# Issuing five of six first loads behind the frame's barriers, and waiting for the last stores on SyncE

## The chip, the core and the metric

The kernel runs on one core of a Trainium2 chip. The metric is the device time of one execution in microseconds; lower is better. Times "before" are from four executions. A profile is one of them, recorded by the hardware profiler; its instants are counted from the first instruction of the program.

## The reference

Attention scores without the softmax: for each of 8 batches and 8 heads, the 512 x 512 products of the rows of q and k (64 long), times 1/8.

```
batch, heads, seq, dim = 8, 8, 512, 64          # float32
scale = 1.0 / np.sqrt(q.shape[-1])
out = np.einsum('bhqd,bhkd->bhqk', q, k) * scale
```

q and k are 8.4 MB each, the output is 67.1 MB.

## The kernel before, in words

The batch is cut into four units of two batches (`UNITS = 4`). For each unit, k and q are loaded whole, 2 MB each, by `load(v, x)` (L77, x = 0 for k, 1 for q), into one of three large buffers `bigs`. GpSimd casts each load to bf16 in two instructions (L119), in the order of the loads, and counts `ready` up once per load. TensorE transposes the cast data in groups of eight tiles (`turn`, L127), VectorE and ScalarE each move half of every group into `kT` and `qz` (`move`, L185). `qz` was filled with zeros by VectorE at the start (L190).

The output is made in 16 pieces of 4 MB (`ALL = 16`, index g). For each, TensorE does eight pairs of matmuls into three PSUM buffers (`scores`, L142), ScalarE (L210) and VectorE (L213) take turns scaling them into one of the three `bigs`, and SyncE issues one store of the whole piece (L96). From the fourth piece on, TensorE waits for the store that used the same buffer three pieces before.

All DMAs are issued by SyncE on one queue, in this order: the six loads of units 0 to 2, the two loads of unit 3 (each after a count of `ready`, L91), and the 16 stores (each after counts of `act` and `dve`, L94 and L95). Each load has its own semaphore; the stores share three.

The instructions are put out by hand, engine by engine. A frame of the scheduler, `tile_critical` (L82), encloses what is issued first. `tc.close()` and `tc.compile()` (L86, L87) end the frame: there all engines meet at barriers. What is written after L87 starts on each engine behind them: GpSimd's identity and casts, VectorE's fills, ScalarE's table load, and SyncE's list from L90 on. At the end of the program one engine waits on the three store semaphores, so that the program does not end before its output has landed.

Of the kernel before, what the change touches and what calls it, by code (L numbers as in the profile page):

```python
# [5 lines left out]
def kernel(  # L6
# [5 lines left out]
    nc = tc.nc  # L12
# [3 lines left out]
    UNITS = B // 2  # L16
# [23 lines left out]
    store_sems = [nc.alloc_semaphore(f"store{n}") for n in range(3)]  # L40
    ALL = CHUNKS * UNITS
# [24 lines left out]
    pe = nc.tensor  # L66
# [3 lines left out]
    def xf(v):  # L70
        return bigs[(0, 1, 2, 1)[v]].rearrange("p x i k -> p (x i k)").rearrange(
            "p (x s c) -> p x s c", x=2, s=2)

    def store_buffer(g):
        return bigs[(0, 2, 1)[g % 3]]

    def load(v, x):  # L77
        nc.sync.dma_start(out=xf(v)[:, x],
                          in_=(k_r, q_r)[x][v].rearrange("p (s c) -> p s c", s=2)
                          ).then_inc(load_sems[2 * v + x], 16)  # L80

    with tc.tile_critical(no_gpsimd_drain=True):  # L82
        for v in range(UNITS - 1):
            for x in range(2):
                load(v, x)
    tc.close()  # L86
    tc.compile()  # L87


    for x in range(2):  # L90
        nc.sync.wait_ge(sem["ready"], 3 + x)  # L91
        load(UNITS - 1, x)
    for g in range(ALL):
        nc.sync.wait_ge(sem["act"], 4 * g + 4)  # L94
        nc.sync.wait_ge(sem["dve"], 4 * g + 4)  # L95
        nc.sync.dma_start(out=out_r[g], in_=store_buffer(g).rearrange("p x i k -> p x (i k)")  # L96
                          ).then_inc(store_sems[g % 3], 16)

    nc.gpsimd.memset(identity, 0.0).then_inc(sem["ident"], 1)  # L99
    nc.gpsimd.wait_ge(sem["ident"], 1)  # L100
# [51 lines left out]
    for g in range(ALL):  # L152
# [7 lines left out]
            scores(g, p)  # L160
        if c < ALL:
            pe.wait_ge(sem["moved"], 4 * c + 4)


    for n in range(3):
        pe.wait_ge(store_sems[n], 16 * len(range(n, ALL, 3)))

# [76 lines left out]
```

## Time and profile before

| what | value |
|---|---|
| median of 4 executions | 201.72 us (201.6 to 201.94) |
| the profiled execution | 201.94 us, span 200.4 us |
| busy share of the span | PE 50%, VectorE 53%, ScalarE 42%, GpSimd 20% |
| moved by DMA | 83.95 MB, mean 419 GB/s |
| six loads of the frame | issued from 0.95 to 3.47 us |
| the last store | issued at 178.05 us, landing in about 22 us |

The span runs from the first to the last instruction of the program; the execution's time has 1.57 us more around it (201.94 less 200.37). In the chain, each row is a piece of work that the next one waited for. A DMA row starts at its issue and ends at its landing, and so includes the time that the transfer stood in the queue behind others. "SPq" and "PEldq" are the sequencers of SyncE and TensorE: their issues, waits and drains.

### The profile page before, as it was taken

To read this page: it belongs to the slowest core of one execution; us is meant where nothing else is said; L and a number is where in the kernel's file an instruction comes from. 1 tells how busy PE (TensorE), PEld (TensorE's weight loads), DVE (VectorE), ACT (ScalarE), POOL (GpSimd) and SP (SyncE) were. 2 spreads that over 40 slices of the span, in tenths; PEclk is the share of its full clock that TensorE was granted. 3 is DMA by queue.
4 is the path that set the end of the run, shared out by engine and by line. 5 is a ranking of instruction groups with operands and counts; after the bars stand their busy time and mean duration, and the time that the engine had idled before them with its cause. 6 is when DMAs were issued, how large, how long until landed. Compare 5 with 4: busy or idle time off the path is not lost.

```text
span 200.4 us, 1081 instructions
## 1 busy us (share of the span) xinstructions
PE 99.4 (50%) x377; PEld 46.7 (23%) x384; DVE 106.2 (53%) x98; ACT 84.9 (42%) x97; POOL 39.5 (20%) x22
## 2 busy tenths in 40 slices
PE   0027550376686638745666666662757573820000
PEld 0026310142433215312333414130212120200000
DVE  0666790075798927692747493947363645450000
ACT  0205760264695726562646464554444443430000
POOL 0399999995000000000000000000000000000000
PEclk9999996588899966997978788899585769695555
DMA  5999999999999999999999999999999999999995
GB/s 186 428 438 425 435 425 438 428 406 435 432 428 425 428 443 430 425 425 442 428 425 425 435 442 425 425 435 435 425 428 428 438 425 422 435 432 428 425 428 242
DMA packets 5509, 83.95 MB, mean 419 GB/s; under 512 B 384, under 2 KB 384, under 8 KB 384
## 3 DMA queue, kind: packets, MB, share of 16 engines
q1 hardware_dynamic: 5504, 83.89, 98.4%
q8 instruction: 3, 0.05, 0.1%
q14 instruction: 2, 0.02, 0.0%
HBM read 16.78 MB, written 67.11 MB: 419 GB/s over the span
## 4 chain that ended last, share of the span: by engine, by line
DMA 53%; DVE 12%; POOL 12%; PE 10%; issue 1%; SPq 0%
DMA out_dram<-big 42%; POOL xb L119 12%; DVE big L213 10%; DMA big<-in_q_dram 7%; PE ps L142 7%; DMA big<-in_k_dram 4%; PE tp L127 3%; DVE qz L185 2%; DVE kT L185 1%; SPq L95 0%; SPq L87 0%; SPq L82 0%
## 5 line engine op out<-in xcount | busy, mean ns | idle before, releaser
L142 PE MATMUL ps<-kT,qz 128*128 128x512 bf16 x249 | 80.3, 457 | 62.4 <-DMA out_dram<-big 30.8
L213 DVE TENSOR_SCALAR big<-ps 128x1024 f32<-128x1024 f32 x64 | 77.1, 1223 | 52.7 <-PE ps L142 49.4
L210 ACT ACTIVATE big<-ps 128x1024 f32<-128x1024 f32 x64 | 65.1, 1025 | 71.9 <-PE ps L142 67.8
L142 PEld LDWEIGHTS ps<-kT,qz 128*128 128x128 bf16 x256 | 25.7, 111 | 110.4 <-DMA out_dram<-big 34.3
L119 POOL CAST xb<-big 128x2048 bf16<-128x2048 f32 x16 | 38.8, 2467 | 3.4 <-DMA big<-in_k_dram 3.1
L127 PE MATMUL tp<-identity,xb 128*128 128x128 f32 x104 | 19.8, 355 | 13.7 <-POOL xb L119 13.7
L127 PEld LDWEIGHTS tp<-identity,xb 128*128 128x128 f32 x104 | 17.9, 190 | 17.6 <-issue 16.3
L185 DVE COPY kT<-tp 64x512 f32<-64x512 f32 x14 | 9.7, 694 | 7.3 <-PE tp L127 6.9
L185 ACT COPY kT<-tp 64x512 f32<-64x512 f32 x14 | 8.1, 579 | 12.1 <-PE tp L127 11.9
L190 DVE MEMSET qz<- 128x4096 uint32 x2 | 6.9, 3472 | 6.7 <-PEq L87 5.9
L185 DVE COPY qz<-tp 64x512 f32<-64x512 f32 x12 | 8.3, 695 | 3.8 <-PE tp L127 3.5
L185 ACT COPY qz<-tp 64x512 f32<-64x512 f32 x12 | 7.4, 615 | 1.8 <-PE tp L127 1.6
L127 PE MATMUL ps<-identity,xb 128*128 128x128 f32 x24 | 3.9, 323 | 1.2 <-POOL xb L119 1.2
L127 PEld LDWEIGHTS ps<-identity,xb 128*128 128x128 f32 x24 | 3.5, 169 | 1.6 <-POOL xb L119 1.6
L185 ACT ACT_TABLE_LOAD x1 | 1.3, 1283 | 4.9 <-PEq L87 4.9
L185 DVE COPY qz<-ps 64x512 f32<-64x512 f32 x4 | 2.8, 695 | 0.9 <-PE ps L127 0.8
L185 ACT COPY qz<-ps 64x512 f32<-64x512 f32 x4 | 2.5, 624 | 1.1 <-PE ps L127 1.1
L185 DVE COPY kT<-ps 64x512 f32<-64x512 f32 x2 | 1.4, 693 | 0.3 <-PE ps L127 0.3
L185 ACT COPY kT<-ps 64x512 f32<-64x512 f32 x2 | 1.2, 579 | 0.5 <-PE ps L127 0.5
L99 POOL MEMSET identity<- 128x128 f32 x1 | 0.2, 205 | 4.5 <-POOLq L87 4.5
L101 POOL TENSOR_SCALAR_AFFINE_SELECT identity<-identity 128x128 f32<-128x128 f32 x1 | 0.3, 294 | 0.2 <-POOL identity L99 0.2
L230 POOL MEMSET const-float32-0.0<- 128x1 f32 x1 | 0.1, 99 | 0.2 <-issue 0.2
(3 smaller groups left out, 0.3 us busy)
## 6 DMA issues: line engine op xcount, KB each, us to landing
out_dram<-big SPq DMA_DIRECT2D x16, 4096.0 KB, 21.6
big<-in_k_dram SPq DMA_DIRECT2D x4, 2048.0 KB, 15.6
big<-in_q_dram SPq DMA_DIRECT2D x4, 2048.0 KB, 17.8
```

The source lines that it names most:

```text
L99: nc.gpsimd.memset(identity, 0.0).then_inc(sem["ident"], 1)
L101: nc.gpsimd.affine_select(out=identity, in_=identity, compare_op=mybir.AluOpType.not_equal, fill=1.0, base=0, pattern=[[-1, P]], channel_m ...
L119: cast = nc.gpsimd.tensor_copy(out=dst, in_=src)
L127: ins = pe.transpose(out=dst[:, w], identity=identity, in_=xw[:, c % SLOTS * W + w])
L142: ins = pe.matmul(out=pss[pair % 3][:, w, :], lhsT=qz[:, n, i + w], rhs=keys[:, n], start=True, stop=True)
L185: copy(out=dst, in_=src[:, h]).then_inc(sem["moved"], 1)
L190: engine.memset(qz[:, v * N:(v + 1) * N], 0.0).then_inc(sem["zeroed"], 1)
L210: lambda o, ps: nc.scalar.mul(out=o, in_=ps, mul=scale),
L213: lambda o, ps: nc.vector.tensor_scalar(out=o, in0=ps, scalar1=scale, scalar2=None, op0=mult),
L230: nc = _bacc.Bacc("TRN2", target_bir_lowering=False, num_devices=1)
```

## The change

Only `load(0, 0)` stays in the frame. The five other early loads are issued by SyncE after L87, in the same order, ahead of the loads of unit 3. The three waits for the last stores are taken from the end of TensorE's list and put at the end of SyncE's, after its last store.

```
     with tc.tile_critical(no_gpsimd_drain=True):
-        for v in range(UNITS - 1):
-            for x in range(2):
-                load(v, x)
+        load(0, 0)
     tc.close()
     tc.compile()
 
 
+    for n in range(1, 2 * (UNITS - 1)):
+        load(n // 2, n % 2)
     for x in range(2):
         nc.sync.wait_ge(sem["ready"], 3 + x)
         load(UNITS - 1, x)
@@ the stores
+    for n in range(3):
+        nc.sync.wait_ge(store_sems[n], 16 * len(range(n, ALL, 3)))
@@ the end of TensorE's list
-    for n in range(3):
-        pe.wait_ge(store_sems[n], 16 * len(range(n, ALL, 3)))
```

## The prediction

> **What bounds the kernel now.** I read the page first, then the chain of waits in order of time, then windows over the first microseconds, then SyncE's issues in order of time, and last the two source lines that the change touches, the end of the scheduler's frame (L87) and the closing waits (L166).
>
> From the page: the span, the DMA share in forty slices of 5.01 us, and the one queue that carries all loads and stores.
>
> ```profile
> span 200.4 us, 1081 instructions
> ...
> DMA  5999999999999999999999999999999999999995
> ...
> q1 hardware_dynamic: 5504, 83.89, 98.4%
> ```
>
> Every slice but the first and the last is full, and no compute engine is over 53% busy. So the kernel is one stream of 83.89 MB, and its time is a start-up, the stream, and an end. The chain (start us, duration us, what) says where both ends are.
>
> ```profile
> 0.95 7.78 DMA big<-in_k_dram
> 8.72 0.05 issue
> 8.78 4.82 POOL xb L119 x2
> ...
> 63.48 19.30 DMA out_dram<-big
> ...
> 90.11 21.96 DMA out_dram<-big
> ...
> 149.15 21.99 DMA out_dram<-big
> ```
>
> The stores that land at 63.48+19.30 = 82.78 and at 90.11+21.96 = 112.07 are three stores of 4.194 MB apart: 12.58 MB in 29.29 us, 430 GB/s. At that rate the stream alone is 83.89/0.430 = 195.1 us of the 200.4. What is left over is 5.3 us, so only the start-up and the end can give anything, unless the stream is broken.
>
> SyncE's issues (start us, duration us, line, transfer) and windows of the start-up (length, then busy us and count of PE, PEld, DVE, ACT, POOL, then clock, DMA share, GB/s):
>
> ```profile
> 0.95 0.38 SPq L78 DMA_DIRECT2D big<-in_k_dram  x1
> 1.38 0.42 SPq L78 DMA_DIRECT2D big<-in_q_dram  x1
> ...
> 3.47 0.47 SPq L78 DMA_DIRECT2D big<-in_q_dram  x1
> 23.44 0.33 SPq L78 DMA_DIRECT2D big<-in_k_dram  x1
> ```
>
> ```profile
> 0.00:2.00 2.00, 0.00 (x0) 0.00 (x0) 0.00 (x0) 0.00 (x0) 0.20 (x4) 1.00 0.09 33
> 2.00:4.00 2.00, 0.00 (x0) 0.00 (x0) 0.00 (x0) 0.00 (x0) 0.00 (x0) 1.00 0.94 238
> 4.00:6.00 2.00, 0.00 (x0) 0.00 (x0) 0.13 (x1) 1.05 (x1) 0.50 (x2) 1.00 0.98 418
> 6.00:8.00 2.00, 0.00 (x0) 0.00 (x0) 2.00 (x1) 0.23 (x1) 0.00 (x0) 1.00 1.01 434
> ```
>
> Data moves from about 1.9 us on (0.09 of 2 us is 0.18 us). From 2 to 4 us the DMA engines are 94% busy but pass 238 GB/s, against 434 later: (430-238) x 2 us = 0.38 MB, or 0.9 us of stream lost. That is also the stretch in which SyncE issues loads 2 to 5.
>
> Frame and end (count, durations in ns min/median/max, first and last start us):
>
> ```profile
> L87 SPq EVENT_SEMAPHORE  x2: 17/17/17, 4.5 to 4.9; - x2
> ...
> L166 PEldq EVENT_SEMAPHORE  x2: 51/4873/9695, 181.0 to 190.7; - x2
> ```
>
> SyncE leaves the barriers at 4.9 us; TensorE's last wait runs from 190.68 for 9.695 us, to 200.37, and it is the last instruction of the program. The landing record of the last store says 200.34: TensorE follows it by 0.03 us. This execution took 201.94 us, so 1.57 us lie outside its span. It is the highest of the four, whose median is 201.72; I sum differences and put them on the median. A difference under 0.2% (0.4 us) is about what a measurement of this kernel cannot tell from none.
>
> **The change part by part.** *Five loads move behind the barriers.* SyncE's last issue in the frame ends at 3.47+0.47 = 3.94 and the barriers at 4.9+0.02, so frame exit and barriers cost SyncE 0.98 us. In the changed kernel load 0 is still issued at 0.95 (nothing ahead of it changes) and ends at 1.33; the other engines wait at the barrier from 0.8 us on, so the barriers end at about 2.3. Loads 1 to 5 follow at the old pitch, (3.47-1.38)/4 = 0.52 us: 2.4, 2.9, 3.4, 4.0, 4.5, done at 4.9. Each comes 1.0 us later than now. Behind them on SyncE stand only the wait for `ready` 3 and the last two loads, at 23.44 and 28.32, so nothing queues up.
>
> Is the stream broken? Load 0 is 2.097 MB, 4.88 us at 430 GB/s; it starts at about 1.9, so it cannot be through before 6.8, and it lands at 0.95+7.78 = 8.73. Load 1 must have data ready by 6.8 at the earliest; from issue to first data load 0 takes 0.95 to 1.9, 1.0 us, so load 1 is ready at 3.4. The cover is 3.4 us, and load 5, needed at 8.73+4x4.88 = 28.2, has over 20. Cost: nothing. If the cover were gone, each microsecond missing would be a microsecond of time.
>
> *Does the 0.9 us lost from 2 to 4 us change?* This the trace of before cannot show, since the first data and the burst of issues come together. Bounds: nothing changes if the loss belongs to the first packets themselves, or if it only moves with the burst to 2.4 to 4.9; -0.9 us if the burst causes it and the later burst finds a stream that is running. An upper end: the window in which load 3,0 is issued (23.44, in a running stream, a single one) keeps 431 GB/s from 20 to 30 us, so an issue costs under 0.1 us there; five of them at most +0.3. I take 0, because the nearest row, that issue in a running stream, shows no price on data and so speaks against the burst as the cause.
>
> *Other engines start 2.6 us earlier.* GpSimd's identity (4.94), ScalarE's table load (4.95) and VectorE's two memsets (5.87 and 10.14, 3.47 each) move to about 2.3, 2.3 and 3.3. None gains: GpSimd's first cast waits for load 0 at 8.73, TensorE's first transposes at 13.7 for that cast pair, and the first evacuation at 15.72 for them. What the casts release, loads 6 and 7 at 23.44 and 28.32, is wanted only when load 5 lands, at about 33.2: 5 us of lead at the least. Store buffers come free by landings, which do not move. Cost 0.
>
> *The closing waits move from TensorE to SyncE.* Instructions: three waits, merged to two in the trace. On TensorE nothing stood behind them. On SyncE they stand behind the last store's issue (178.05, 0.37 us), with nothing behind them either. The last landing stays at 200.34, SyncE's semaphore instructions take 17 ns against 51, so the span ends within 0.05 us of now. What follows the last instruction, inside those 1.57 us, no row shows by engine. Today SyncE's share of it is run from 178.4 on, under 22 us of store, and TensorE's is exposed; afterwards the other way round. Bounds: -0.3 us if TensorE's is the longer by some ten semaphore steps of 34 ns; +0.6 us if SyncE has one more round of the kind that L87 shows (from its drain at 4.31 to 4.92). I take 0, since the rows nearest to it, single semaphore and drain instructions of 7 to 55 ns, are far under the resolution.
>
> [...]
>
> "DMA: Bandwidth & Descriptors", section "Rules for kernel authors", says to issue a DMA early and wait for it late, which speaks against delaying five loads; by that rule alone the change would cost up to 1.0 us, 202.7. The row of load 0 (landing 8.73, with load 1 issued at 2.4) decides against it here.
>
> Sum: 0 + 0 + 0 + 0 on 201.72: **201.7 us**.
>
> **The rivals.** *SyncE's end is longer (slower).* One mechanism: work behind the last instruction on SyncE that now hides under the last store is exposed. It decides from 0.4 us on; by the barrier row it is +0.4 to +0.7: 202.1 to 202.4. For it: 1.57 us lie outside the span, and SyncE is the engine with the queue. Against: single instructions there take tens of ns.
>
> *The start-up loss goes (faster).* The five issues caused the 0.9 us between 2 and 4 us, and with load 0 alone in the queue until 2.4 a good half is saved: -0.4 to -0.9, 200.8 to 201.3. For it: 94% busy at 238 GB/s, just while SyncE issues, and full rate from when it stops at 3.94. Against: the single issue at 23.44, without a dent, and the first packets would be slow in any case.
>
> *The change does not do what it says:* if SyncE were held in the frame until load 0 lands, load 1 would come at 9.5 and the stream would stop for over 1.5 us: above 203.2. Against: in the trace its drains there take 7 to 55 ns with six loads in flight.
>
> **How the numbers follow.** No change that can be told: 0.46. SyncE's longer end: 0.27. Start-up loss gone: 0.19. A held SyncE: 0.02. The rest, 0.06, is drift of the slowest DMA engine (the 16 parts of the last store land from 198.3 to 200.34, and the last one sets the time), split 0.04 faster and 0.02 slower. So faster 0.23, same 0.46, slower 0.31. The middle case alone is 201.3 to 202.1. The range takes in most of both rivals, 201.0 to 202.4, leaving out about 1 in 10 on each side.
>
> **What would show it right or wrong.** Right: load 0 at 0.95, loads 1 to 5 from about 2.4 to 4.9, casts still from 8.7 on, the last store's issue within 0.5 us of 178, a span of 200.2 to 200.6 ended by SyncE's wait. Wrong by the start: the window from 2 to 4 us well above 300 GB/s and the first cast before 8.3. Wrong by the end: the same span but more than 1.57+0.4 us outside it. A gap in the DMA share in the first two slices would mean that the cover of 3.4 us was miscounted.

## The result and the profile after

The changed kernel takes 201.45 us (median of 41 runs, 201.27 to 201.79), the kernel before 201.68 us (61 runs, 201.56 to 202.01). The ratio is 0.9987, 95% interval 0.9983 to 0.9992: faster by 0.13%, clear of noise over so many runs and inside the 0.2% that the prediction called no change. What is to be explained is 0.23 us.

The profiled execution took 201.78 us. Its page, lines that answer to those of before:

```profile
span 200.5 us, 1081 instructions
...
DMA  5999999999999999999999999999999999999995
...
q1 hardware_dynamic: 5504, 83.89, 98.4%
```

The span is not shorter (200.47 us against 200.37). The stream is as full as before. The chain of waits of the changed kernel (start us, duration us, what):

```profile
0.95 7.82 DMA big<-in_k_dram
8.76 0.05 issue
8.82 4.81 POOL xb L122 x2
...
148.52 22.71 DMA out_dram<-big
```

Load 0 is issued at the same instant, and the first cast starts 0.04 us later than before. SyncE's issues, and the window from 2 to 4 us:

```profile
0.95 0.39 SPq L78 DMA_DIRECT2D big<-in_k_dram  x1
2.34 0.34 SPq L78 DMA_DIRECT2D big<-in_q_dram  x1
...
4.29 0.46 SPq L78 DMA_DIRECT2D big<-in_q_dram  x1
23.46 0.33 SPq L78 DMA_DIRECT2D big<-in_k_dram  x1
```

```profile
2.00:4.00 2.00, 0.00 (x0) 0.00 (x0) 0.74 (x1) 1.28 (x1) 0.50 (x2) 1.00 0.96 254
```

Loads 1 to 5 come from 2.34 to 4.75, and the DMA engines still pass only 254 GB/s at 96% busy. Last, the closing waits, now on SyncE (count, ns min/median/max, first and last start in us):

```profile
L99 SPq EVENT_SEMAPHORE  x2: 17/4852/9686, 181.1 to 190.8; - x2
```

The second wait runs from 190.781 for 9.686 us, to 200.467, 0.02 us after the last landing at 200.444. What has changed is the time outside the span: 201.78 less 200.467 is 1.31 us, against 1.57 before. That is no accident of one run: over 42 runs of the changed kernel, the profiled one included, the time less the span is 1.305 us in the mean (1.26 to 1.38, with spans given to 0.1 us), and the mean span is 200.17. In 27 runs of the kernel before it is 1.576 (1.52 to 1.64), with a mean span of 200.18. So the 0.23 us lie outside the span.

### The profile page after: what moved, and what is told of

The parts are those of the page before. It is cut to its first block, busy times and chain, and to the rows that moved or that the text cites. A ratio compares the mean times of both kernels' runs of the same rounds, so it can differ in the third digit from the quotient of the medians.

```text
span 200.5 us, 1081 instructions
## 1 busy us (share of the span) xinstructions
PE 101.0 (50%) x377; PEld 48.0 (24%) x384; DVE 106.0 (53%) x98; ACT 84.8 (42%) x97; POOL 39.5 (20%) x22
## 4 chain that ended last, share of the span: by engine, by line
DMA 54%; POOL 12%; DVE 12%; PE 10%; issue 1%; SPq 0%
DMA out_dram<-big 43%; POOL xb L122 12%; DVE big L212 9%; PE ps L145 8%; DMA big<-in_q_dram 7%; DMA big<-in_k_dram 4%; PE tp L130 2%; DVE qz L184 2%; DVE kT L184 1%; SPq L95 0%; SPq L85 0%; SPq L82 0%
## 5 line engine op out<-in xcount | busy, mean ns | idle before, releaser
L130 PE MATMUL tp<-identity,xb 128*128 128x128 f32 x104 | 19.3, 348 | 13.8 <-POOL xb L122 13.8
L130 PE MATMUL ps<-identity,xb 128*128 128x128 f32 x24 | 5.6, 423 | 1.2 <-POOL xb L122 1.2
L130 PEld LDWEIGHTS ps<-identity,xb 128*128 128x128 f32 x24 | 5.0, 229 | 1.6 <-POOL xb L122 1.6
```

The lines of the kernel that those rows point to most:

```text
L130: ins = pe.transpose(out=dst[:, w], identity=identity, in_=xw[:, c % SLOTS * W + w])
```

## The experiments

Theory A: only the closing waits count; the engine that waits last decides how much time lies outside the span, taken to be behind the last instruction. Rival B: the loads count, through the start or what lies ahead of the first instruction, since the frame is shorter.

**One part alone: the loads.** From the changed kernel, the waits go back to TensorE.

```
-    for n in range(3):
-        nc.sync.wait_ge(store_sems[n], 16 * len(range(n, ALL, 3)))
...
+    for n in range(3):
+        pe.wait_ge(store_sems[n], 16 * len(range(n, ALL, 3)))
```

> Only the loads are moved; TensorE waits for the last stores as before. Theory A (the 0.23 us came from the end, behind the last instruction; the move of the loads is worth nothing): 201.6 to 201.8, with 1.55 to 1.60 us outside the span, as before. Rival B (the gain comes from the start, or from what lies ahead of the first instruction because the frame is shorter): 201.4 to 201.5, with about 1.3 us outside the span or a span shorter by 0.2. Rival C (half and half): 201.55, 1.43 outside.

Measured: 201.67 us (11 runs), before 201.73 in the same job, ratio 0.9994 (0.9986 to 1.0003). Outside the span 1.575 us in the mean.

**The other part alone: the waits.** From the kernel before, the three waits move from TensorE to the end of SyncE's list; all six loads stay in the frame.

```
+    for n in range(3):
+        nc.sync.wait_ge(store_sems[n], 16 * len(range(n, ALL, 3)))
...
-    for n in range(3):
-        pe.wait_ge(store_sems[n], 16 * len(range(n, ALL, 3)))
```

> All six loads stay in the frame; SyncE waits for the last stores. Theory A: 201.4 to 201.5, with 1.3 us outside the span. Rival B: 201.6 to 201.8, 1.57 outside. Rival C: 201.55, 1.43 outside.

Measured: 201.45 us (11 runs), ratio 0.9985 (0.9977 to 0.9994), outside 1.320 us. Both runs came out as theory A had them: the waits alone give the time of the changed kernel to 0.01 us, the loads alone 0.06 us, which the interval does not tell from nothing. Rivals B and C fall. The closing waits of the kernel with the loads alone:

```profile
L166 PEldq EVENT_SEMAPHORE  x2: 51/4873/9695, 180.7 to 190.4; - x2
```

TensorE's wait starts at 190.41 and ends this span at 200.11, 0.04 us after the last landing at 200.07; the execution's time is 201.67, so 1.56 us are left outside, as before, although the start is that of the changed kernel.

**Is the start-up loss the burst's?** The prediction had 0.9 us of stream lost between 2 and 4 us, and a rival in which the burst of issues caused it.

```
-    for n in range(1, 2 * (UNITS - 1)):
+    nc.sync.wait_ge(sem["ident"], 2)
+    load(0, 1)
+    nc.sync.wait_ge(load_sems[0], 16)
+    for n in range(2, 2 * (UNITS - 1)):
         load(n // 2, n % 2)
```

> As the changed kernel, but load 1 is issued only after GpSimd's identity is made (about 3.1 us) and loads 2 to 5 only when load 0 has landed (8.8 us), so that one issue in place of three to five falls between 2 and 4 us. If the burst of issues causes the start-up loss: the window from 2 to 4 us shows over 350 GB/s and the time is 200.5 to 201.0. If the loss belongs to the first packets themselves: 230 to 270 GB/s in that window as in both kernels, and 201.4 to 201.5, no change against the changed kernel.

Measured: 201.47 us (11 runs), ratio to before 0.9986 (0.9977 to 0.9994): the time of the changed kernel. Its issues and its windows:

```profile
0.95 0.39 SPq L78 DMA_DIRECT2D big<-in_k_dram  x1
3.09 0.34 SPq L78 DMA_DIRECT2D big<-in_q_dram  x1
8.71 0.33 SPq L78 DMA_DIRECT2D big<-in_k_dram  x1
```

```profile
2.00:4.00 2.00, 0.00 (x0) 0.00 (x0) 0.74 (x1) 1.28 (x1) 0.50 (x2) 1.00 0.93 229
4.00:6.00 2.00, 0.00 (x0) 0.00 (x0) 2.00 (x1) 0.00 (x0) 0.00 (x0) 1.00 0.99 426
```

With one issue in that window in place of four, its rate does not rise (229 GB/s, against 238 before and 254 in the changed kernel), and it is full from 4 us on as in both kernels. The burst is not the cause; that rival falls. Where the loss sits, the packet records show: a window counts each packet, 16 KB here, at its start, and in the changed kernel the first 16 packets take 1.31 us each in the mean, against 0.61 for nearly all that follow.

**The cover taken away.** Loads 1 to 5 wait for the landing of load 0.

```
+    nc.sync.wait_ge(load_sems[0], 16)
     for n in range(1, 2 * (UNITS - 1)):
         load(n // 2, n % 2)
```

> As the changed kernel, but loads 1 to 5 are issued only when load 0 has landed (8.8 us). This takes away the cover of 3.4 us that the prediction counted. Load 1 is issued at 8.8, its data starts at about 9.8, and the stream stands from about 8.0: 1.8 us lost if a restart runs at full rate at once (203.2 to 203.4); 2.7 us lost if every start from rest loses the 0.9 us again (204.0 to 204.3). If the stream were not the bound: no change, 201.45.

Measured: 204.33 us (4 runs), ratio to before 1.0127 (1.0111 to 1.0142), 2.88 us over the changed kernel. Its chain, and windows of two microseconds from the first data on and from the restart on:

```profile
0.95 7.58 DMA big<-in_k_dram
8.54 0.34 SPq L78
8.88 0.05 issue
8.94 12.22 DMA big<-in_k_dram
21.16 0.05 issue
21.21 4.87 POOL xb L123 x2
```

```profile
1.90:3.90 2.00, 0.00 (x0) 0.00 (x0) 0.64 (x1) 1.28 (x1) 0.50 (x2) 1.00 1.00 254
9.50:11.50 2.00, 0.00 (x0) 0.00 (x0) 1.51 (x1) 0.00 (x0) 2.00 (x2) 1.00 1.10 254
```

Load 1 is issued at 8.54. By the packet records the last data of load 0 ends at 8.2 and that of load 1 starts at 9.52. The two windows are the first two microseconds of data after each rest: 254 GB/s both times, at a DMA share of 1.00 and 1.10. Load 2 lands at 21.16 in place of 18.52, 2.64 us later, although load 0 landed 0.24 us earlier than in the changed kernel. The second expectation (2.7 us) is the nearer one, and the time lies just above its 204.0 to 204.3: a start from rest loses nearly a microsecond each time ((430-254) x 2 us = 0.35 MB, 0.8 us). That loss and the 1.3 us from 8.2 to 9.52 do not yet make 2.64. The 16 DMA engines do not stop at one instant: the last 16 packets of load 0 end between 7.59 and 8.20, at 7.93 in the mean, and the first 16 of load 1 start at 9.66 in the mean, a rest of 1.73 us. Those 16 take 1.45 us each, and the first 48 together cost 1.03 us per engine over the usual 0.61 us a packet. The sum is 2.76 us. With the quiet start, which shows the same loss without the burst, it goes to the start itself; why the first packets take so long is open.

**Which engine waits last.** Two theories of the 0.26 us: each engine's own step speed, or its place in a closing round. Each kernel is the changed one with SyncE's three waits moved to the end of the named engine's list; for ScalarE:

```
-    for n in range(3):
-        nc.sync.wait_ge(store_sems[n], 16 * len(range(n, ALL, 3)))
...
+    for n in range(3):
+        nc.scalar.wait_ge(store_sems[n], 16 * len(range(n, ALL, 3)))
```

> As the changed kernel, but ScalarE waits for the last stores in place of SyncE. Two theories of the 0.26 us that lie outside the span with TensorE and not with SyncE (1.57 against 1.31 us). Step speed: each engine runs the same closing steps, and TensorE's are slow (51 ns against 17 for one semaphore step); ScalarE, with 17 ns, then comes like SyncE: 1.28 to 1.34 us outside, 201.4 to 201.5. Place in the closing round: the engines pass a token in a fixed order, and the time depends on where the last one stands; ScalarE then lies apart from SyncE by a multiple of one hop, 1.36 to 1.52 or under 1.25 us outside, 201.5 to 201.65 or under 201.4.

> As the changed kernel, but VectorE waits for the last stores. Step speed: 21 ns a step against 17, so 1.30 to 1.37 us outside the span, 201.4 to 201.55. Place in the closing round: a value of its own, different from those of SyncE, ScalarE and GpSimd by 0.04 us or more.

> As the changed kernel, but GpSimd waits for the last stores. Step speed: 17 ns a step as on SyncE, 1.28 to 1.34 us outside the span, 201.4 to 201.5. Place in the closing round: a value of its own, as for the two others; with TensorE at one end (1.57) and SyncE at the other (1.31), the five values then form a ladder with steps of about 0.065 us.

| last wait on | time, us (runs) | against before | outside the span, mean (lowest to highest) |
|---|---|---|---|
| SyncE (changed kernel) | 201.45 (41) | 0.9987 (0.9983 to 0.9992) | 1.305 (1.26 to 1.38) |
| VectorE | 201.56 (10) | 0.9994 (0.9984 to 1.0003) | 1.403 (1.37 to 1.44) |
| ScalarE | 201.55 (10) | 0.9994 (0.9985 to 1.0004) | 1.472 (1.42 to 1.52) |
| TensorE (loads alone) | 201.67 (11) | 0.9994 (0.9986 to 1.0003) | 1.575 (1.52 to 1.64) |
| GpSimd | 201.96 (10) | 1.002 (1.001 to 1.0031) | 1.849 (1.80 to 1.89) |

The median spans of the five lie between 200.10 and 200.15, so the difference is in the last column (42 runs for SyncE, with the profiled one), and it separates the engines where the times alone overlap. The waits themselves, on ScalarE and on GpSimd:

```profile
L215 ACTq EVENT_SEMAPHORE  x2: 17/4856/9695, 180.8 to 190.5; - x2
```

```profile
L215 POOLq EVENT_SEMAPHORE  x2: 17/4852/9686, 180.7 to 190.4; - x2
```

Both engines take 17 ns for a semaphore step, like SyncE, and are 0.17 and 0.54 us dearer. Step speed falls. The round fits only in part: four engines stand on a ladder (1.31, 1.40, 1.47, 1.57), but GpSimd stands far above it, not between as its expectation had it. That the engine which waits last decides the time outside the span is shown; why each has its price is not. That this time lies behind the last instruction and not ahead of the first is argued: the moved waits touch nothing at the start, but the trace has no instruction on either side of the span.

**The first issue's price.** The frame is left out, and load 0 stands with the other five behind the barriers.

```
-    with tc.tile_critical(no_gpsimd_drain=True):
-        load(0, 0)
     tc.close()
     tc.compile()
...
-    for n in range(1, 2 * (UNITS - 1)):
+    for n in range(0, 2 * (UNITS - 1)):
```

> As the changed kernel, but the frame is left out and load 0 stands with the other five at the head of SyncE's list. Theory (the stream bounds, so the time follows the first issue one to one, and nothing else at the start counts): the time is 201.45 plus the shift of the first issue from 0.95 us. Without the frame's own steps (0.72 to 0.95 on SyncE) but behind one barrier pass of the kind that L85 shows (about 0.55 us), the first issue should come at 1.2 to 1.4, and the time at 201.7 to 201.9; if the barriers go with the frame, at 0.75 and 201.25. If a hidden cost of the frame counted besides, the time would fall by more than the shift of the first issue says.

Measured: 201.88 us (11 runs), ratio to before 1.0009 (1.0000 to 1.0018).

```profile
1.39 0.39 SPq L78 DMA_DIRECT2D big<-in_k_dram  x1
1.83 0.42 SPq L78 DMA_DIRECT2D big<-in_q_dram  x1
```

The first issue comes at 1.39 in place of 0.95, 0.44 us later, and the time is 0.43 us over the changed kernel: one to one, within the interval of 0.2 us to either side. So at the start the instant of the first issue counts, and nothing else of the frame that these runs can tell. No version that beats the changed kernel came out of the runs.

## Why the prediction held, and where it did not

*The five loads.* Held: issues from 2.34 (2.4 foretold) to 4.75 (4.9), load 0 unmoved, stream unbroken. The cover was real, though its 3.4 us were not measured: load 1 issued at 2.34 (loads alone) or at 3.09 (quiet start) costs nothing that can be told, and issued at 8.54 the time rises by 2.88 us. The rule of the Trainium skill that the prediction sets beside this term, up to 1.0 us for issuing later, did not show within that cover. The prediction was short in one point: it said that each missing microsecond costs one. A gap costs its length and a start-up loss besides.

*The 0.9 us from 2 to 4 us.* Taken at 0, and rightly: the quiet start shows 229 GB/s there. The reason given, that a single issue in a running stream leaves no dent, pointed the right way. Its upper end was added wrongly: five issues at under 0.1 us are at most 0.5, not 0.3; nothing hung on it.

*The other engines' earlier start.* Worth nothing, as foretold: the first cast starts at 8.82 against 8.78, and the mean span is the same.

*The closing waits.* This is the term that was mis-sized. It was bounded by -0.3 and +0.6 and taken at 0; it is -0.26, nearly the lower bound. The choice rested on single semaphore steps of 7 to 55 ns as the nearest rows. But 1.57 us behind and ahead of a span are not one step, and the trace held nothing on how they differ by engine; the likelier value of such a term is not 0 only because its rows are small. The price of the lower bound, ten slow steps of TensorE, came near the size by luck: the runs on ScalarE and GpSimd refute its reason. The slower rival, that SyncE's end is longer, looked in the right place, outside the span, with the wrong sign: of the five engines tried SyncE's is the shortest.

The Trainium skill, "Runtime: NRT & Kernel Launch", section "The ~15µs preamble/postamble breakdown", gives about 0.355 us, eight hops of 44 ns, for the pass of the barrier over five engines ahead of a kernel; for the barrier behind it, it gives no hops. If the closing pass were like the opening one, which is an estimate and which no run here shows, TensorE against SyncE, 0.26 us, would lie within it; GpSimd against SyncE, 0.54, would not, so such a pass alone could not be all of it.

*The number.* 201.7 was foretold on the 201.72 shown then; 201.45 was measured, and the difference is that one term. No change was the right call because the term stayed under the 0.4 us taken as telling; over 41 and 61 runs the interval is about 0.1 us to either side, so the sign of the term could be seen. One sign was set too tight: the last store's issue, within 0.5 us of 178, came at 178.64. With the loads alone it came at 177.65, so this instant differs between profiles by more than the sign allowed.

## What to carry to other kernels

In a kernel that one DMA stream fills from end to end, look first at the instant of the first issue, at gaps, and at what follows the last landing. Issues moved within the cover of a running transfer were free here, and the cover is counted from the two issues and the transfer's length. Compare the time outside the span as well as the span: here it held the whole gain, and the span alone would have said no change. Try which engine holds the last wait, since the five differed here by up to 0.54 us.

## What the runs showed of the hardware that was not expected

- The engine that waits last sets the time outside the span: 1.31 us on SyncE, 1.40 on VectorE, 1.47 on ScalarE, 1.57 on TensorE, 1.85 on GpSimd.
- Each start of the DMA stream from rest loses about 0.8 to 1.0 us: 254 GB/s in the first two microseconds (1.90 to 3.90 in the changed kernel, 9.50 to 11.50 after the gap) against 430 later, with the DMA engines busy. The loss sits in the first packets, 1.31 and 1.45 us in the mean for the first 16 of 16 KB against 0.61 later. One issue in the window from 2 to 4 us in place of four made no difference to it.
